# Local attention scores: the queries' remaining parts against the keys' leading parts only, two heads on the two halves of the array's rows

## Chip, cores and metric

The kernel runs on one core of a Trainium2 chip. The metric is the device time of one execution in microseconds (us). A program's time is the median of its runs; beside it stands one profiled execution, in which every instruction has its start and its length.

## What is computed

The reference is a two-layer encoder trunk over 2048 tokens of width 1024. Layer 0 mixes windowed attention (8 query heads of 64, 2 key heads, window of 128 to both sides, a sink logit and a distance bias) with a short convolution; layer 1 mixes latent attention with a gated MLP. The change lies in layer 0's windowed attention alone, in this line and the one that follows it:

```python
logits = jnp.einsum('bnqkgd,bnskd->bnkgqs', qb, kw).astype(jnp.float32) * (dh ** -0.5)
logits = logits - slopes * dist[:, :, None, None]
```

For each block n of 128 queries and each key head g, four query heads meet the keys of three blocks (384 keys; 256 for the first and the last block).

## The kernel before

**Split numbers.** A float32 value is held as two float32r parts: the leading part (a copy in float32r) and the remaining part (the difference). The helper `split` (L66 to L69) makes them, on ScalarE and VectorE. A product of two such values is made on TensorE as three matmuls (`mm3`, L78 to L80): leading with leading, leading with remaining, remaining with leading.

**Scores.** A head has only 64 numbers, so the scores are packed differently. The keys' tile `kw` holds the 64 leading rows on partitions 0 to 63 and the 64 remaining rows on partitions 64 to 127 (L397). The queries' tile `qw` holds, for each of four heads, the leading part (index a = 0) and the remaining part (a = 1), each of them twice, on both halves of the partitions (L393 to L395). One matmul over all 128 rows with a = 0 gives leading times (leading + remaining); a second one with a = 1 gives remaining times (leading + remaining), all four products. Both go into the same PSUM bank (L401 to L404):

```python
for j in range(4):
    ps = self.psB("ps")
    for a in range(2):
        nc.tensor.matmul(ps[:, :W], q[:, a, j], k[:, :W], start=a == 0, stop=a == 1)
```

The queries are the stationary operand (128 columns), the keys the moving one (W = 384 or 256 columns). VectorE then adds the distance bias while it takes the bank out to `L` (L406). `psB` has two banks.

**Stage A.** `phase_a` projects the input in 24 column tiles of weights by four chunks of 512 tokens: each such unit is 24 matmuls of 512 columns (`project`, with `mm3`). After a unit, `attend` traces the attention of one (n, g) at a time, with a priority that puts it ahead: the output matmuls of the pair two before (`att_out`, L441), the transposes of the pair one before (`att_turn`, L429), the scores of this one (`att_scores`). There are 32 pairs of (n, g). A scheduler fixes each engine's order when the program is built; an engine then runs its instructions in that order and waits where an operand or a buffer isn't ready. The SP queue issues nearly all of the stage's transfers, also in a fixed order.

**After it.** `phase_out(0)` makes the output projection of layer 0; it needs what stage A wrote to DRAM as `u0`. Layer 1 follows. None of its code changes.

Of the kernel before, what the change touches and what calls it, by code (L numbers as in the profile page):

```python
# [12 lines left out]
F32R = mybir.dt.float32r  # L13
I32 = mybir.dt.int32
AF = mybir.ActivationFunctionType
ALU = mybir.AluOpType
# [4 lines left out]
P = 128  # L21
# [33 lines left out]
class Builder:  # L55
# [116 lines left out]
    def phase_a(self):  # L172
        tc, nc, I, c, d = self.tc, self.nc, self.i, self.c, self.d
# [5 lines left out]
        sp = es.enter_context(tc.tile_pool(name="aat", bufs=1))  # L179
# [192 lines left out]
        def att_scores(n, g):  # L372
            k0 = max(0, (n - 1) * P)
            k1 = min(S, (n + 2) * P)
            W = k1 - k0
            off = k0 - (n - 1) * P
            if g == 0:
                b = blk[n] = {}
                kp = sp.tile([P, 2, 3 * P], F32, name="kp", tag="kp", bufs=1)
                self.dma(kp[:, 0, :W], d["posh"][k0:k1].partition_broadcast(P))  # L380
                self.dma(kp[:, 1, :W], d["posl"][k0:k1].partition_broadcast(P))
                dist = sp.tile([P, 3 * P], F32, name="dist", tag="dist", bufs=2)
                nc.vector.tensor_scalar(dist[:, :W], kp[:, 1, :W], posq[:, 1, n:n + 1], None, ALU.subtract)
                nc.vector.scalar_tensor_tensor(dist[:, :W], kp[:, 0, :W], posq[:, 0, n:n + 1], dist[:, :W],
                                               ALU.subtract, ALU.add)
                nc.scalar.activation(dist[:, :W], dist[:, :W], AF.Abs)
                nc.gpsimd.tensor_tensor(dist[:, :W], dist[:, :W], mask[:, off:off + W], ALU.add)
                b.update(dist=dist, W=W)
                b["o"] = sp.tile([P, 4, P], F32, name="oT", tag="oT", bufs=2)
            b = blk[n]  # L390


            q = sp.tile([P, 2, 4, P], F32R, name="qw", tag="qw", bufs=2)  # L393
            for a in range(2):
                self.dma(q[64 * a:64 * a + 64], d["q0"][64 * g:64 * g + 64, n])  # L395
            k = sp.tile([P, 3 * P], F32R, name="kw", tag="kw", bufs=2)
            self.dma(k[:, :W], d["k0"][g].rearrange("a e s -> (a e) s")[:, k0:k1])  # L397
            v = b["v", g] = sp.tile([P, 3, P], F32R, name="vw", tag="vw", bufs=4)
            self.dma(v[:, :W // P], d["v0"][k0:k1, g].rearrange("(b p) a e -> p b (a e)", p=P))
            L = b["L", g] = sp.tile([P, 4, 3 * P], F32, name="L", tag="L", bufs=2)  # L400
            for j in range(4):  # L401
                ps = self.psB("ps")
                for a in range(2):
                    nc.tensor.matmul(ps[:, :W], q[:, a, j], k[:, :W], start=a == 0, stop=a == 1)  # L404
                slope = 2.0 ** -(4 * g + j + 1)
                nc.vector.scalar_tensor_tensor(L[:, j, :W], b["dist"][:, :W], -8.0 * slope, ps[:, :W],  # L406
                                               ALU.mult, ALU.add)
            sm = sp.tile([P, 6, 4], F32, name="sm", tag="sm", bufs=3)
            nc.vector.tensor_reduce(sm[:, 0], L[:, :, :W], AX.X, ALU.max)
            nc.vector.tensor_tensor(sm[:, 0], sm[:, 0], sink8[:, 4 * g:4 * g + 4], ALU.max)  # L410
            nc.vector.tensor_scalar(sm[:, 1], sm[:, 0], -0.125, None, ALU.mult)
            nc.vector.tensor_tensor(sm[:, 2], sink[:, 4 * g:4 * g + 4], sm[:, 1], ALU.add)
            nc.scalar.activation(sm[:, 2], sm[:, 2], AF.Exp)
            for j in range(4):
                nc.scalar.activation(L[:, j, :W], L[:, j, :W], AF.Exp, bias=sm[:, 1, j:j + 1], scale=0.125,
                                     accum_out=sm[:, 3, j:j + 1])
            nc.vector.tensor_tensor(sm[:, 4], sm[:, 3], sm[:, 2], ALU.add)
            nc.vector.reciprocal(sm[:, 5], sm[:, 4])
            for j in range(4):
                nc.vector.tensor_scalar(L[:, j, :W], L[:, j, :W], sm[:, 5, j:j + 1], None, ALU.mult)  # L420
# [49 lines left out]
        def attend(limit):  # L470
            t = tick[0]
            if t >= len(groups) + 2 or (t < len(groups) and groups[t][0] >= limit):
                return False
            tick[0] += 1
            with tc.high_priority(ATTEND):
                if t >= 2:
                    att_out(*groups[t - 2])
                if 1 <= t <= len(groups):
                    att_turn(*groups[t - 1])
                if t < len(groups):  # L480
                    att_scores(*groups[t])
            return True
# [986 lines left out]
```

## Time and profile before

| | us |
|---|---|
| median of 3 runs | 2878.97 (2873.27 to 2884.52) |
| the profiled execution | 2881.51 |
| its span, first to last instruction | 2879.7 |
| TensorE busy, of the span | 2819.8 (98%) |
| VectorE busy | 1987.6 (69%) |
| ScalarE busy | 1322.2 (46%) |
| GpSimd busy | 1096.7 (38%) |

Engines: PE is TensorE's matmuls, PEld its weight loads (they run beside the matmuls), DVE VectorE, ACT ScalarE, POOL GpSimd, SPq the DMA-issuing queue of SyncE. Matmuls are pipelined and the end of each is modelled, so that the lengths of matmuls in a row overlap: what one costs is read from start to start, not from its length. In a timeline "x4" joins neighbours of one kind, and the length is that of all.

### The profile page before, as it was taken

The page shows a single profiled execution, that of the slowest core. Times are in us where ns is not written, and L with a number is a line of the kernel's source. Part 1 is how long each engine was busy: PE and PEld are TensorE (multiplying, and loading weights), DVE is VectorE, ACT ScalarE, POOL GpSimd, SP SyncE. Part 2 cuts the span into 40 slices and gives each one's busy share as a digit, 9 for nine tenths or more (in the row PEclk, how much of TensorE's full clock was granted, in tenths as well). Part 3 has the DMA queues.
Part 4 walks back from the last instruction along what each step waited for, and adds up shares of the span by engine and source line. Part 5 has one row for each costly group of instructions (what it writes and reads, how often), then busy time and mean ns, then how long its engine had stood idle before and what let it go on. Part 6 is the DMA issues. An engine that isn't in the chain of part 4 may idle for free. (4 is left out here: it accounts for less than half of the span.)

```text
span 2879.7 us, 38354 instructions
## 1 busy us (share of the span) xinstructions
PE 2819.8 (98%) x12808; PEld 2292.0 (80%) x12808; DVE 1987.6 (69%) x3957; ACT 1322.2 (46%) x2475; POOL 1096.7 (38%) x833
## 2 busy tenths in 40 slices
PE   9999999999999999999999999999999999899999
PEld 7888888888788887888887877777777776678887
DVE  4688557786655554454764789989898995666665
ACT  3545335445211111324442368888888887211111
POOL 0011000022311111120102258898899888523432
PEclk9999999999999999999999999999999999899999
DMA  7644365453733445423873333133322323433441
GB/s 233 186 139 140 124 194 166 133 142 118 219 119 119 130 136 212 148 66 128 292 268 108 106 101 76 37 72 84 84 54 61 83 69 78 139 106 114 126 123 43
DMA packets 316598, 365.26 MB, mean 127 GB/s; under 512 B 33248, under 2 KB 244368, under 8 KB 311280
## 3 DMA queue, kind: packets, MB, share of 16 engines
q1 hardware_dynamic: 249056, 295.62, 36.6%
q10 hardware_dynamic: 67344, 67.18, 7.0%
q8 instruction: 101, 1.65, 0.2%
q14 instruction: 97, 0.79, 0.1%
HBM read 238.19 MB, written 124.53 MB: 126 GB/s over the span
## 5 line engine op out<-in xcount | busy, mean ns | idle before, releaser
L1334 POOL TENSOR_TENSOR acc<-acc,ph 128x512 f32<-128x512 f32 x448 | 582.9, 1302 | 41.8 <-ACT ph L1326 10.9
L1328 DVE TENSOR_TENSOR pl<-pst,ph 128x512 fp32r<-128x512 f32 x512 | 347.0, 684 | 62.7 <-ACT ph L1326 50.0
L1196 DVE TENSOR_REDUCE mx<-pm 128x1 f32<-128x512 f32 x512 | 347.8, 682 | 27.4 <-PE pm L1195 21.1
L78 PE MATMUL pa<-xh,w 128*128 128x512 f32 x832 | 328.4, 395 | 6.0 <-ACT xh L68 6.0
L79 PE MATMUL pa<-xl,w 128*128 128x512 f32 x832 | 329.9, 397 | 0.0
L80 PE MATMUL pa<-xh,w 128*128 128x512 f32 x832 | 328.0, 394 | 0.0
L1323 ACT ACTIVATE pst<-pst 128x512 f32<-128x512 f32 x512 | 296.6, 585 | 61.2 <-PE pst L1322 29.9
L1326 ACT ACTIVATE ph<-pst 128x512 fp32r<-128x512 f32 x512 | 301.5, 595 | 31.8 <-POOL acc L1334 1.6
L78 PE MATMUL py<-wh,ou 128*128 128x512 f32 x512 | 208.3, 407 | 13.0 <-DVE ox L639 8.2
L1320 PE MATMUL pst<-mqh,mkh 97*128 97x512 f32 x512 | 205.6, 402 | 3.6 <-DVE pl L1328 1.9
L1195 PE MATMUL pm<-mkh,mqh 96*128 96x512 f32 x512 | 203.3, 398 | 4.8 <-DVE mx L1196 4.8
L647 POOL TENSOR_TENSOR ox<-ox,ln_g 128x1024 f32<-128x1024 f32 x32 | 80.4, 2514 | 334.3 <-DMA praw<-in_pT 171.6
L90 PE MATMUL pg<-wh,oht 128*128 128x512 f32 x512 | 201.1, 393 | 4.5 <-ACT oht L68 4.5
L1245 PE MATMUL px<-ph,mv 128*128 128x512 f32 x512 | 205.3, 401 | 0.0
L79 PE MATMUL py<-wl,ou 128*128 128x512 f32 x512 | 205.3, 401 | 0.0
L1321 PE MATMUL pst<-mql,mkh 96*128 96x512 f32 x512 | 204.4, 399 | 0.0
L1322 PE MATMUL pst<-mqh,mkl 96*128 96x512 f32 x512 | 203.8, 398 | 0.0
L80 PE MATMUL py<-wh,ou 128*128 128x512 f32 x512 | 203.6, 398 | 0.0
L1246 PE MATMUL py<-pl,mv 128*66 128x512 f32 x512 | 201.9, 394 | 0.8 <-DVE pl L1328 0.7
L90 PE MATMUL pg<-wl,oht 128*128 128x512 f32 x512 | 200.4, 391 | 0.0
L671 ACT ACTIVATE osg<-pg 128x512 f32<-128x512 f32 x64 | 38.3, 599 | 344.8 <-PE pg L92 333.2
L78 PEld LDWEIGHTS pa<-xh,w 128*128 128x128 f32 x832 | 157.4, 189 | 37.8 <-ACT xh L68 7.0
(370 smaller groups left out, 6255.3 us busy)
## 6 DMA issues: line engine op xcount, KB each, us to landing
ou<-u SPq DMA_DIRECT2D x96, 256.0 KB
qw<-q SPq DMA_DIRECT2D x64, 256.0 KB
x1T<-oxt ACTq DMA_DIRECT2D x64, 256.0 KB
cx<-x1T SPq DMA_DIRECT2D x16, 1024.0 KB
q<-st SPq DMA_DIRECT2D x32, 256.0 KB
u<-ua SPq DMA_DIRECT2D x32, 256.0 KB
wraw<-in_w_out SPq DMA_DIRECT2D x16, 512.0 KB
ox<-in_x SPq DMA_DIRECT2D x16, 512.0 KB
```

The lines of the kernel that those rows point to most:

```text
L78: mm(ps, ah, bh, start=start, stop=False)
L79: mm(ps, ah, bl, start=False, stop=False)
L80: return mm(ps, al, bh, start=False, stop=stop)
L90: mm(ps, a[:, 0, k], b[k][part][:, cols], start=k == 0 and part == 0, stop=False)
L1196: nc.vector.tensor_reduce(self.mx[blk][:, b, kc:kc + 1], ps, AX.X, ALU.max)
L1245: mm(x, v[:, kb, 0:P], ph, start=kb == 0, stop=kb == 15)
L1320: mm(ps, kh[0:97, ks], qh[0:97, qs], start=True, stop=False)
L1321: mm(ps, kh[0:96, ks], ql[0:96, qs], start=False, stop=False)
L1323: ex = nc.scalar.activation(ps, ps, AF.Exp, scale=scale)
L1326: nc.scalar.activation(ph, ps, AF.Copy)
L1328: behind = nc.vector.tensor_tensor(pl, ps, pf, ALU.subtract)
L1334: nc.gpsimd.tensor_tensor(acc, acc, pf, ALU.add)
```

## The change

For a pair of heads, two PSUM banks are taken together. Two full matmuls (128 rows) come first, one for each head, as before: leading queries against both parts of the keys. Then come two matmuls of 64 rows each: the first head's remaining parts on rows 0 to 63 against the keys' leading parts in `kw`, the second head's on rows 64 to 127 against a second copy of the keys' leading parts, in a new tile `kw2`. The product remaining by remaining is left out. The four are kept in this order on TensorE, and the two evictions follow. One transfer is added for each (n, g): 64 partitions of `kw2`.

```diff
             k = sp.tile([P, 3 * P], F32R, name="kw", tag="kw", bufs=2)
             self.dma(k[:, :W], d["k0"][g].rearrange("a e s -> (a e) s")[:, k0:k1])
+            k2 = sp.tile([P, 3 * P], F32R, name="kw2", tag="kw2", bufs=2)
+            self.dma(k2[64:128, :W], d["k0"][g, 0, :, k0:k1])
             v = b["v", g] = sp.tile([P, 3, P], F32R, name="vw", tag="vw", bufs=4)
...
-            for j in range(4):
-                ps = self.psB("ps")
-                for a in range(2):
-                    nc.tensor.matmul(ps[:, :W], q[:, a, j], k[:, :W], start=a == 0, stop=a == 1)
-                slope = 2.0 ** -(4 * g + j + 1)
-                nc.vector.scalar_tensor_tensor(L[:, j, :W], b["dist"][:, :W], -8.0 * slope, ps[:, :W],
-                                               ALU.mult, ALU.add)
+            for j2 in range(0, 4, 2):
+                pss = [self.psB("ps") for _ in range(2)]
+                with tc.manual_schedule(engines={mybir.EngineType.PE}):
+                    for j, ps in enumerate(pss):
+                        nc.tensor.matmul(ps[:, :W], q[:, 0, j2 + j], k[:, :W], start=True, stop=False)
+                    for j, (ps, kk) in enumerate(zip(pss, (k, k2))):
+                        r = slice(64 * j, 64 * j + 64)
+                        nc.tensor.matmul(ps[:, :W], q[r, 1, j2 + j], kk[r, :W], start=False, stop=True)
+                for j, ps in zip((j2, j2 + 1), pss):
+                    slope = 2.0 ** -(4 * g + j + 1)
+                    nc.vector.scalar_tensor_tensor(L[:, j, :W], b["dist"][:, :W], -8.0 * slope, ps[:, :W],
+                                                   ALU.mult, ALU.add)
```

## Rows read from the trace of the kernel before

**Rows 1.** The page: span, busy time of TensorE, granted clock in 40 slices.

```profile
span 2879.7 us, 38354 instructions
...
PE 2819.8 (98%) x12808; PEld 2292.0 (80%) x12808; DVE 1987.6 (69%) x3957; ACT 1322.2 (46%) x2475; POOL 1096.7 (38%) x833
...
PEclk9999999999999999999999999999999999899999
```

**Rows 2.** Windows, first to last score matmul: length, busy us (instructions), clock, DMA share, GB/s.

```profile
76.00:680.00 604.00, 601.74 (x2895) 505.55 (x2895) 442.12 (x844) 287.66 (x619) 73.54 (x69) 1.00 0.52 149
```

**Rows 3.** Waits of PE from 0 to 720 us: waiter, cause, total us, times, longest.

```profile
PE pa L78 <- ACT xh L68: 6.0, 2, 5.0
PE ps L404 <- DMA kw<-k: 2.3, 1, 2.3
```

**Rows 4.** Timeline of PE, one narrow and one wide stretch: start, length, instruction.

```profile
76.97 0.64 PE L404 MATMUL ps<-kw,qw 128*128 128x256 f32 x4
77.44 0.39 PE L80 MATMUL pa<-xh,w 128*128 128x512 f32 x1
...
134.71 0.39 PE L78 MATMUL pa<-xh,w 128*128 128x512 f32 x1
134.94 0.85 PE L404 MATMUL ps<-kw,qw 128*128 128x384 f32 x4
135.64 0.39 PE L79 MATMUL pa<-xl,w 128*128 128x512 f32 x1
135.87 0.40 PE L80 MATMUL pa<-xh,w 128*128 128x512 f32 x1
```

**Rows 5.** The score matmuls by tile: lengths in ns (min/median/max), first and last start, forms.

```profile
L404 PE MATMUL ps<-kw,qw x256: 274/336/687, 77.0 to 671.3; 128*128 128x384 f32 x112, 128*128 128x256 f32 x16
```

**Rows 6.** Timeline of PE around a block of transposes (L429).

```profile
156.10 0.28 PE L523 MATMUL cs<-ones,sqa 128*128 128x2 f32 x2
156.24 1.07 PE L429 MATMUL pt<-ident,L 128*128 128x128 f32 x8
157.07 0.48 PE L79 MATMUL pa<-xl,w 128*128 128x512 f32 x1
157.38 0.39 PE L80 MATMUL pa<-xh,w 128*128 128x512 f32 x1
157.61 0.40 PE L78 MATMUL pa<-xh,w 128*128 128x512 f32 x1
```

**Rows 7.** Timeline of PE in layer 1: matmuls of 97 and 96 rows behind 128.

```profile
1900.63 0.39 PE L1246 MATMUL py<-pl,mv 128*66 128x512 f32 x1
1900.86 0.40 PE L1320 MATMUL pst<-mqh,mkh 97*128 97x512 f32 x1
1901.10 0.40 PE L1321 MATMUL pst<-mql,mkh 96*128 96x512 f32 x1
```

**Rows 8.** Timeline of DVE: evictions of the scores (L406) and what stood between.

```profile
135.49 0.55 DVE L406 SCALAR_TENSOR_TENSOR L<-dist,ps 128x384 f32<-128x384 f32 x1 [0.26 <-PE ps L404]
135.96 1.22 DVE L69 TENSOR_TENSOR w<-w_12r,w 128x1024 fp32r<-128x1024 f32 x1
137.10 0.55 DVE L406 SCALAR_TENSOR_TENSOR L<-dist,ps 128x384 f32<-128x384 f32 x1
```

**Rows 9.** Timeline of the SP queue: start of an issue, its length, transfer.

```profile
147.35 1.09 SPq L74 DMA_DIRECT2D qw<-q  x2
148.49 0.58 SPq L74 DMA_DIRECT2D kw<-k  x1
151.12 0.56 SPq L74 DMA_DIRECT2D szw<-sza  x1
```

**Rows 10.** Timeline of PE at the end of stage A.

```profile
715.52 0.39 PE L80 MATMUL pa<-xh,w 128*128 128x512 f32 x1
715.75 4.74 PE L523 MATMUL cs<-ones,sqb 128*128 128x2 f32 x32
722.86 0.77 PE L78 MATMUL py<-wh,ou 128*128 128x512 f32 x1 [2.37 <-DMA ou<-u]
```

## The prediction

> **What bounds the kernel now.** I read the page first. TensorE is busy for 2819.8 of 2879.7 us, with its clock granted in full nearly throughout [rows 1]; no other engine comes near. Then the stretch that holds every score matmul, 76 to 680 us: PE is busy for 601.74 of 604 us at clock 1.00 [rows 2]. A busy share can hide short stalls, since the lengths of matmuls are modelled and overlap, so the waits come next: up to 720 us PE is seen waiting 6.0 us for a split of the input and 2.3 us for the keys, and for nothing else [rows 3]. So the stage is as long as TensorE's instruction stream. What is taken out of that stream is won, unless a wait takes its place; what happens on other engines costs nothing as long as PE doesn't come to wait for it. The stage's end is PE's too: projections run until 715.52, the closing column sums start right behind, and the next stage starts at 722.86, 2.37 us of it a wait for a transfer [rows 10]. A shift of PE's stream moves this end along with it.
>
> **What a score matmul costs.** From start to start, not by length. Four wide ones run from 134.94 to 135.64, so 175 ns each; four narrow ones from 76.97 to 77.44, so 117 ns each [rows 4]. Their modelled length is 336 ns at the median [rows 5], so some 161 ns of one lie over its successor. A (n, g) has eight of them; 28 of the 32 (n, g) are wide, 4 narrow.
>
> **The change, part by part.**
>
> *The leading queries' matmuls* stay as they are, four for each (n, g).
>
> *The remaining parts.* Four full matmuls become two pairs of half matmuls, with as many columns each. If the two of a pair run beside each other, a pair takes the time of one: 175 ns saved for each of 56 wide pairs, 117 ns for each of 8 narrow ones: 9.8 + 0.9 = 10.7 us. If they run one behind the other, nothing is saved: a matmul of 96 or 97 rows starts its successor 0.24 us later, just as long as one with 128 [rows 7], so fewer rows alone buy nothing. The trace of before has no matmul on a part of the rows beside another, so the term lies between 0 and -10.7 us. I take overlap, because the two share no array rows, no partitions and no bank, and what they do share, the issue and the weight loading, is short in the trace: two small matmuls with weights of their own start 0.14 us before the next kind, 70 ns each [rows 6]. In Part 3, The mechanism, of the page TensorE: Matmul & The Clock Gate, the Trainium skill says that matmuls on different row groups overlap and start about 4 ns apart; no row of before shows it, and by it the term would be within 0.3 us of its full 10.7.
>
> *One weight load more in the time of a matmul.* Eight transposes with a weight load each start within 0.83 us, 104 ns each [rows 6], and this I take for what a load needs. Two loads for a pair are 208 ns, the matmul over which they can be made lasts 175 ns, so 33 ns stick out: 64 pairs by 33 ns, +2.1 us. If the second load can't start before the first half runs, the second half starts 104 ns late, and the pair saves 71 instead of 142 ns, some 4.5 us in all; if loads hide entirely, the term is 0.
>
> *Changing the array's shape.* Going from full rows to halves and back happens once for each pair, 64 times in and 64 times out, because projections stand on both sides. The nearest rows: 97 and 96 rows behind 128 cost nothing (0.23 to 0.24 us) [rows 7]; the first projection behind a block of transposes takes 0.31 us to its successor instead of 0.23, 80 ns more [rows 6]; and if the pipeline had to run empty at each change, the 161 ns that now lie over the successor would show. So 0, 80 or 161 ns at a change. I take 80 ns once for each pair, since a change of matmul kind is nearer to this than fewer rows in the same kind: +5.1 us; the ends are 0 and 128 by 161 ns, +20.6 us.
>
> Against the change speaks the Trainium skill, TensorEngine Tiling, Key Properties: changing the tiling mode, not just the tile, drains TensorE. No row of before changes the mode, so none bears it out; it is the second rival below.
>
> *Two banks at once.* The second pair of a (n, g) needs both banks free, so two evictions of 0.55 us each must be done, where before one sufficed for the next head. Queued behind the waiting matmul on PE are projections, and everything that they feed. I cost this at nothing, because the scheduler puts projections between the pairs, as it does now (six of them, 1.4 us, fit over two evictions), and the trace shows no wait of PE for a bank [rows 3]. The cover fails where VectorE is late: in [rows 8] a weight split of 1.22 us stands between two evictions. That is the third rival.
>
> *VectorE* has the same 128 evictions: nothing.
>
> *The added transfer.* 32 issues on the SP queue, each some 0.58 us as that of `kw` [rows 9], put `vw` and whatever follows back by that much. The queue has room (nothing is issued from 149.07 to 151.12 [rows 9]), its buffer comes free with those of `kw`, and the DMA engines are 0.52 busy [rows 2]. PE waited once for `kw`, 2.3 us [rows 3]; the new tile is issued 0.6 us later but is needed two matmuls (0.35 us) later. Nothing, with 0 to +3 us as bounds, the top being that one wait come again.
>
> *Order.* A new program has a new fixed order on each engine. That can win or lose a few us at stage borders; the whole of the stage's visible waits is 8.3 us [rows 3], so I allow 4 us either way.
>
> **The sum.** -10.7 + 2.1 + 5.1 = -3.5 us. On the profiled execution's 2881.51 us that is 2878.0. That execution lies 2.5 us above the median of the runs, so against the median 2878.97 the forecast is 2875.5 us. A measurement of this kernel can tell about 0.5% from no change, 14.4 us; the forecast is well within.
>
> **The rivals.**
>
> 1. *The halves run one behind the other.* The change then doesn't do what it says: no matmul time is saved, and the change of shape stays. +5.1 us, 2884 us (2879 to 2892). For it: nothing in the trace of before shows two matmuls at once, and every form, whatever its rows, has its full price. Against it: they share no rows and no bank.
>
> 2. *Overlap, but the array runs empty at each change of shape.* -10.7 + 2.1 + 20.6 = +12.0 us, 2891 us. It turns the change into a loss from (10.7 - 2.1)/128 = 67 ns at a change. For it: the 80 ns behind the transposes show that a change of kind isn't always free. Against it: 96 rows behind 128 are free.
>
> 3. *PE waits for the second bank.* The second pair stands in PE's order where the scheduler thought both banks free; if VectorE is late by one eviction (0.55 us) in each of the 32 (n, g), that is 17.6 us, and with the forecast's -3.5 the time is 2893 us. Over +14.4 us it comes if PE waits 0.56 us for each (n, g). Against it: today's PE waits for no bank.
>
> 4. *Slower: no overlap and an array that runs empty.* +20.6 us, 2900 us. This is one mechanism, TensorE treating a half as a full matmul in another mode; at full price for the halves it passes +14.4 us from 112 ns at each of the 128 changes. For and against: as in 1 and 2 together.
>
> **How the numbers follow.** Forecast 0.45; halves in a row 0.22; overlap with emptying 0.13; waits for banks 0.10; no overlap with emptying 0.10. More than 14.4 us faster is out of the sum's reach (10.7 is its most), and only a luckier order adds to it: 0.05, taken from the forecast. More than 14.4 us slower: most of the last case (0.09), half of the waits (0.05), a small part of the second rival (0.03): 0.17. The rest, 0.78, is within 0.5%. The range reaches from full overlap with all else free, 2868, less 4 for the order, to the last case: 2864 to 2900. About 1 in 10 is left out at each end.
>
> **What the profile after would show.** *Overlap*: the two half matmuls of a pair start within some 35 ns, and the next projection starts about 0.2 us after the first; in a row, they start 175 ns apart. *Weights*: a weight load of the second half that ends behind the end of the full matmul's columns. *Change of shape*: the start of the first half stands more than 175 ns behind that of the second full matmul, or the projection after the pair takes over 0.23 us to its successor; 80 ns a pair is my term, 161 ns on both sides the rival's. *Banks*: PE waiting for DVE at the score matmuls, absent now. *The transfer*: PE waiting for `kw2`. *Through to the end*: stage A's last projection, 715.52 now, comes earlier by what the pairs save, and the later stages keep their lengths. The prediction is wrong if the score matmuls are cheaper by 10 us and the time isn't, or if stages that the change doesn't touch differ by more than 4 us.

## The result, and the profile after

The changed kernel takes 2897.62 us at the median of 4 runs (2893.79 to 2900.64), the kernel before 2876.12 beside it: ratio 1.0072, 95% interval [1.0057, 1.0088]. That is a loss of some 21 us, over the 0.5% that can be told from no change, where "no change" was forecast.

The page of the changed kernel, the lines that answer to [rows 1]:

```profile
span 2892.0 us, 38411 instructions
...
PE 2833.7 (98%) x12808; PEld 2277.8 (79%) x12808; DVE 1994.8 (69%) x3957; ACT 1322.6 (46%) x2475; POOL 1098.8 (38%) x833
...
PEclk9999999999999999999999999999999999899999
```

TensorE is as full as before, its clock as high, with the same number of matmuls; its weight loads are busy 14 us less. The waits of PE explain nothing either. Those up to 740 us, as in [rows 3]:

```profile
PE pa L78 <- ACT xh L68: 6.3, 3, 5.1
PE pvt L313 <- ACT st L310: 1.4, 1, 1.4
```

There is no wait for a bank and none for `kw2` or `kw`. Yet the stage is longer. Its end on PE, as in [rows 10]:

```profile
732.89 0.39 PE L80 MATMUL pa<-xh,w 128*128 128x512 f32 x1
733.12 3.63 PE L531 MATMUL cs<-ones,sqb 128*128 128x2 f32 x32
740.69 0.77 PE L78 MATMUL py<-wh,ou 128*128 128x512 f32 x1 [3.94 <-DVE wl L69]
```

The column sums begin at 733.12 instead of 715.75, 17.4 us later, and layer 0's output projection 17.8 us later. So the loss arises in stage A.

Not all of the 17.4 us can be the half matmuls'. The score matmuls in the changed kernel:

```profile
L408 PE MATMUL ps<-kw,qw x128: 275/332/422, 80.0 to 694.1; 128*128 128x384 f32 x112, 128*128 128x256 f32 x16
L411 PE MATMUL ps<-kw,qw x128: 379/440/443, 80.3 to 694.3; 64*128 64x384 f32 x112, 64*128 64x256 f32 x16
```

The first score starts at 80.0 us, where the kernel before has 77.0 [rows 5]. So 3 us are gone before any half runs; on the other side the wait of 2.3 us for the keys [rows 3] is gone from the stretch of the scores. What the halves cost is better read against a full-row kernel with the same frame (run 2 below).

Of the two profiled executions the one after is 12.3 us longer, 2893.79 against 2881.51: from the column sums to the end it is 2164 us before and 2159 after, and 2159 to 2168 in those experiments below whose attention ends with the stage, so the stages behind, which the change doesn't touch, differ by that much from one program to the next.

Where the loss arises shows in TensorE's timeline around one pair of heads (L408 are the full matmuls, L411 the halves). A passage from full rows to half rows and back is called a visit from here on.

```profile
140.06 0.40 PE L78 MATMUL pa<-xh,w 128*128 128x512 f32 x1
140.30 0.33 PE L408 MATMUL ps<-kw,qw 128*128 128x384 f32 x1
140.56 0.44 PE L411 MATMUL ps<-kw,qw 64*128 64x384 f32 x2
140.93 0.50 PE L79 MATMUL pa<-xl,w 128*128 128x512 f32 x1
141.27 0.40 PE L80 MATMUL pa<-xh,w 128*128 128x512 f32 x1
141.50 0.85 PE L449 MATMUL po<-PT,vw 128*128 128x512 f32 x3
```

The two halves, joined in one row, last 0.44 us together, and one alone has a median of 440 ns (line L411 above): they run beside each other. In the trace's own records the starts of a pair are 3 to 4 ns apart. But from the full matmul to the halves it is 0.26 us, where 0.17 is its own time [rows 4]; from the halves to the next projection 0.37; and from that to its successor 0.34, where it is 0.23 elsewhere [rows 6]. The weight loads of the same place say why:

```profile
140.07 0.19 PEld L408 LDWEIGHTS ps<-kw,qw 128*128 128x128 f32 x1
140.56 0.19 PEld L411 LDWEIGHTS ps<-kw,qw 64*128 64x128 f32 x2 [0.30 <-issue]
140.93 0.19 PEld L79 LDWEIGHTS pa<-xl,w 128*128 128x128 f32 x1 [0.18 <-issue]
141.04 0.19 PEld L80 LDWEIGHTS pa<-xh,w 128*128 128x128 f32 x1
141.27 0.66 PEld L449 LDWEIGHTS po<-PT,vw 128*128 128x128 f32 x3
```

Elsewhere a load starts a whole matmul ahead of its use, as the one at 140.07 does for the matmul at 140.30, and the one at 141.04 for that at 141.27. Here the halves' loads start only at 140.56, together with the halves and 0.07 us before the full matmul's modelled end, and the next projection's only at 140.93, 0.07 us before the halves' end. So it is at all 71 visits of this trace, wide and narrow: the first load behind a change starts 1 to 3 ns ahead of the matmul that needs it. No load crosses the change of shape, in either direction. The list of waits does show it, not for PE but for PEld, in a row that the kernel before doesn't have (19.7 us over 68 loads of halves):

```profile
PEld ps L411 <- issue: 19.7, 68, 0.4
```

Taking 0.104 us for a load [rows 6]: going in, 0.26 - 0.17 = 0.09 us pass beyond the full matmul's own time until the halves' load starts, and I take this for the array running empty; then 0.10 of loading stands bare (it lies in the halves' recorded length, 0.44 instead of 0.33). Going out, it is 0.37 - 0.10 - 0.17 = 0.10 us of emptying and the next load's 0.11. That is 0.39 to 0.40 us for one visit, against 0.174 us that a pair saves. The sum and the starts of the loads are read from the trace; the split between emptying and loading is an estimate from these rows.

### The profile page after: what moved, and what is told of

Its sections match the earlier page's. It is cut to its first block, busy times and chain, and to the rows that moved or that the text cites. A ratio compares the mean times of both kernels' runs of the same rounds, so it can differ in the third digit from the quotient of the medians.

```text
span 2892.0 us, 38411 instructions
## 1 busy us (share of the span) xinstructions
PE 2833.7 (98%) x12808; PEld 2277.8 (79%) x12808; DVE 1994.8 (69%) x3957; ACT 1322.6 (46%) x2475; POOL 1098.8 (38%) x833
## 5 line engine op out<-in xcount | busy, mean ns | idle before, releaser
L78 PE MATMUL py<-wh,ou 128*128 128x512 f32 x512 | 208.0, 406 | 17.8 <-DVE ox L647 11.5
```

What stands on the lines that cost most here:

```text
L78: mm(ps, ah, bh, start=start, stop=False)
```

## The experiments

The theory: the price lies in the change of shape, once for each visit. The rivals: the two banks, the order or the added transfer make TensorE wait; or each half matmul is dear by itself.

**1. Full rows in the changed kernel's frame.**

```diff
-                    for j, (ps, kk) in enumerate(zip(pss, (k, k2))):
-                        r = slice(64 * j, 64 * j + 64)
-                        nc.tensor.matmul(ps[:, :W], q[r, 1, j2 + j], kk[r, :W], start=False, stop=True)
+                    for j, ps in enumerate(pss):
+                        nc.tensor.matmul(ps[:, :W], q[:, 1, j2 + j], k[:, :W], start=False, stop=True)
```

> The changed kernel with its two banks at once, its fixed order of four matmuls and its transfer of kw2, but the remaining queries' matmuls on all 128 rows again, against both parts of the keys. Theory (changes of the array's shape cost about 0.4 us a pair of halves, 64 pairs): without half matmuls the loss goes, the time is that of before, ratio 0.999 to 1.002, and the last projection of stage A ends near 716 us. Rival (taking two banks at once, or the added transfer, makes TensorE wait): the loss stays, ratio 1.006 to 1.008, last projection near 733 us.

Measured: 2893.68 us, ratio 1.0052 [1.0039, 1.0064]. By its number that is the rival's. But the time went at another place. This run's first score starts only at 88.8 us, 11.8 us later than in the kernel before, and up to 80 us PE waited for weights (second row), which it does neither before [rows 3] nor after:

```profile
PE pvt L313 <- ACT st L310: 3.6, 1, 3.6
PE pa L78 <- ACT w L68: 3.1, 1, 3.1
```

The SP queue of this run:

```profile
28.86 2.53 SPq L74 DMA_DIRECT2D kw<-k  x4
...
50.75 0.59 SPq L74 DMA_DIRECT2D w_4r<-in_w  x1
...
63.57 0.55 SPq L74 DMA_DIRECT2D w_5r<-in_w  x1
```

In the kernel before, `w_5r` is issued at 30.84. With no reader, `kw2` never holds its buffer, so its loads (shown as `kw` too; digits are left off the names) were free to go early, and at attention's priority they went ahead of the weights. The control was at fault, and its time tells nothing of the change.

**2. The control mended.** `kw2` is a full copy of `kw`, and the second head's remaining matmul reads it.

```diff
-            self.dma(k2[64:128, :W], d["k0"][g, 0, :, k0:k1])
+            self.dma(k2[:, :W], d["k0"][g].rearrange("a e s -> (a e) s")[:, k0:k1])
...
-                        r = slice(64 * j, 64 * j + 64)
-                        nc.tensor.matmul(ps[:, :W], q[r, 1, j2 + j], kk[r, :W], start=False, stop=True)
+                        nc.tensor.matmul(ps[:, :W], q[:, 1, j2 + j], kk[:, :W], start=False, stop=True)
```

> The full-row control again, with what was wrong in the first one mended: there kw2 had no reader, so its buffers were free at once and its loads were issued ahead of weight loads (TensorE lost some 12 us before 80 us). Here kw2 is a full copy of kw (128 partitions) that the second head's remaining matmul reads, all on 128 rows, in the changed kernel's two banks and order. Theory (the loss is the change of shape): as before, ratio 0.998 to 1.003, excess of TensorE's stream in stage A, over matmuls at their start-to-start times, some 18 us as in before, last projection near 716 to 720 us. Rival (two banks, order or transfer): ratio 1.005 to 1.008.

Measured: 2878.67 us, ratio 1.0002 [0.9993, 1.0011]. The end of its stage A:

```profile
714.22 0.39 PE L80 MATMUL pa<-xh,w 128*128 128x512 f32 x1
714.46 3.63 PE L530 MATMUL cs<-ones,sqb 128*128 128x2 f32 x32
```

Two banks at once, the fixed order and a transfer twice as large as the change's cost nothing that shows in the time (the interval reaches from -0.07% to +0.11%). So the loss belongs to the matmuls on half rows. Against this kernel, whose first score starts at 79.3 us, the changed kernel's stage A is 18.7 us longer (733.12 against 714.46), 0.7 of it ahead of the first score and some 17.9 behind it.

**3. Full rows without `kw2`**: the edit of 1, and

```diff
-            k2 = sp.tile([P, 3 * P], F32R, name="kw2", tag="kw2", bufs=2)
-            self.dma(k2[64:128, :W], d["k0"][g, 0, :, k0:k1])
```

> Full rows, two banks at once and the fixed order, without kw2 and its transfer. Theory: as before, ratio 0.998 to 1.003. If the first control's loss was the two banks after all and not the unread kw2, it is there again: 1.004 to 1.006.

Measured: 2878.53 us, ratio 1.0008 [0.9997, 1.0020]. It agrees, and shows that the first control's loss was the unread tile's.

**4. One half instead of two.**

```diff
-                    for j, (ps, kk) in enumerate(zip(pss, (k, k2))):
-                        r = slice(64 * j, 64 * j + 64)
-                        nc.tensor.matmul(ps[:, :W], q[r, 1, j2 + j], kk[r, :W], start=False, stop=True)
+                    nc.tensor.matmul(pss[0][:, :W], q[:, 1, j2], k[:, :W], start=False, stop=True)
+                    nc.tensor.matmul(pss[1][:, :W], q[64:128, 1, j2 + 1], k2[64:128, :W], start=False, stop=True)
```

> The changed kernel with only the second head's remaining part on 64 rows; the first head's is a full matmul ahead of it. As many changes of shape, but half as many half matmuls, and nothing beside them. Theory (the halves overlap fully, the price belongs to the change of shape): 64 matmuls of 175 or 117 ns more, +10.7 us over the changed kernel, ratio to before 1.010 to 1.012. Rival (the price belongs to each half matmul, about 0.2 us each over a full one, without overlap): half of them gone, ratio 1.003 to 1.004.

Measured: 2906.13 us, ratio 1.0092 [1.0079, 1.0105]; stage A's column sums begin at 742.88, 9.8 us after those of the changed kernel. One visit with a lone half:

```profile
150.38 0.34 PE L409 MATMUL ps<-kw,qw 128*128 128x384 f32 x1
150.65 0.43 PE L410 MATMUL ps<-kw,qw 64*128 64x384 f32 x1
151.01 0.50 PE L78 MATMUL pa<-xh,w 128*128 128x512 f32 x1
151.35 0.39 PE L79 MATMUL pa<-xl,w 128*128 128x512 f32 x1
```

0.27, 0.36 and 0.34 us: a lone half takes what a pair takes. The second half is free, and the price is the visit's. Fewer half matmuls made the kernel slower, which the price for each half excludes. The median lies somewhat under the theory's 1.010 to 1.012: the changed kernel turned out to make more than 64 visits and to overlap fewer than 64 pairs (below run 8). And of the 9.8 us some 2.3 are again gone before the first score, which starts at 82.3 here.

**5. The halves apart**, full, half, full, half.

```diff
-                    for j, ps in enumerate(pss):
-                        nc.tensor.matmul(ps[:, :W], q[:, 0, j2 + j], k[:, :W], start=True, stop=False)
                     for j, (ps, kk) in enumerate(zip(pss, (k, k2))):
                         r = slice(64 * j, 64 * j + 64)
+                        nc.tensor.matmul(ps[:, :W], q[:, 0, j2 + j], k[:, :W], start=True, stop=False)
                         nc.tensor.matmul(ps[:, :W], q[r, 1, j2 + j], kk[r, :W], start=False, stop=True)
```

> The changed kernel with the four matmuls of a pair in the order full, half, full, half: the same instructions, twice as many changes of shape, no overlap. Theory (0.4 us for each change in and out, and the halves' overlap lost): a pair takes some 1.49 us instead of 0.93, 64 times 0.57 is +36 us over the changed kernel, ratio to before 1.018 to 1.021. Rival (price of each half matmul, not of the change): only the overlap is lost, if there was one, 0 to +11 us over the changed kernel, ratio 1.007 to 1.011.

Measured: 2935.17 us, ratio 1.0192 [1.0178, 1.0205], as the theory has it: with twice the visits the loss is more than doubled.

**6. Four heads in one visit**, with two banks borrowed from tag C.

```diff
-            for j2 in range(0, 4, 2):
-                pss = [self.psB("ps") for _ in range(2)]
+            for j2 in (0,):
+                pss = [self.psB("ps"), self.psB("ps"), self.psC("ps"), self.psC("ps")]
...
-                    for j, (ps, kk) in enumerate(zip(pss, (k, k2))):
-                        r = slice(64 * j, 64 * j + 64)
+                    for j, (ps, kk) in enumerate(zip(pss, (k, k2, k, k2))):
+                        r = slice(64 * (j % 2), 64 * (j % 2) + 64)
```

> The changed kernel with all four heads of a (n, g) together: four full matmuls into four banks (two of tag B, two of tag C), then the four half matmuls, so one change in and out where there were two. Theory: 32 times 0.4 us less, -12.7 us against the changed kernel, ratio to before 1.000 to 1.004; no better than that, since one change (0.40 us) costs what two overlapped pairs save (0.35 us). Rival (price of each half matmul): as the changed kernel, 1.006 to 1.008. If holding four banks makes TensorE wait, that shows as idle time of PE ahead of the score matmuls, transposes or output matmuls.

Measured: 2954.70 us, ratio 1.0260 [1.0239, 1.0281]: neither. Its scores end here:

```profile
L411 PE MATMUL ps<-kw,qw x128: 277/437/687, 80.4 to 804.7; 64*128 64x384 f32 x112, 64*128 64x256 f32 x16
```

The last projection starts at 713.83, and the scores ran on until 804.7 with little to cover them (before, they end at 671.3 [rows 5]). I put this down to the banks taken from transposes and outputs, which this run alone doesn't show; the question of the price needed banks of its own.

**7 and 8. Four banks of their own**: the kernel of 6 with these edits, and for the control (8) also with the edit of 2, full rows.

```diff
-        self.c_bufs = 3
+        self.a_bufs, self.b_bufs, self.c_bufs = 2, 4, 2
...
+        self.a_bufs, self.b_bufs, self.c_bufs = 3, 2, 3
+        self.ps_open("psx")
...
-                pss = [self.psB("ps"), self.psB("ps"), self.psC("ps"), self.psC("ps")]
+                pss = [self.psB("ps"), self.psB("ps"), self.psB("ps"), self.psB("ps")]
```

> Four heads together again, four full matmuls and four halves, but with four banks of their own: in stage A tag A has 2 banks, B 4, C 2, and a new pool with 3, 2 and 3 opens for the stages behind. Attention then need not share tag C's banks, which put it off beyond the stage's projections in the run before. Theory (0.40 us for each change in and out, 32 of them): +2 us against full rows in the same banks (the next kernel); rival (a price of some 0.2 us for each half matmul): +15 us against it.

> The same four banks with all eight score matmuls on 128 rows (kw2 a full copy, read by the second and fourth head): the control for the four banks. Two projection banks instead of three could cost some us; ratio to before 0.999 to 1.004. By the theory the kernel with halves in these banks is 2 us (0 to 4) slower than this one, by the rival some 15 us.

Measured: with halves 2924.93 us, ratio 1.0162 [1.0148, 1.0177]; with full rows 2912.08, 1.0116 [1.0103, 1.0130]. The second misses its own expectation, 0.999 to 1.004: attention falls behind the projections in these banks too, where tag C still has one bank less than in the kernel before. Its last projection starts at 709.20, its last scores far behind:

```profile
L410 PE MATMUL ps<-kw,qw x128: 277/337/422, 84.9 to 732.5; 128*128 128x384 f32 x112, 128*128 128x256 f32 x16
```

The difference between the two is 12.9 us, near the rival's 15 and not the theory's 2. The timeline of the kernel with halves shows what I had overlooked:

```profile
149.96 0.68 PE L408 MATMUL ps<-kw,qw 128*128 128x384 f32 x3
150.57 0.43 PE L411 MATMUL ps<-kw,qw 64*128 64x384 f32 x1
150.93 0.50 PE L449 MATMUL po<-PT,vw 128*128 128x512 f32 x1
151.27 0.60 PE L437 MATMUL pt<-ident,L 128*128 128x128 f32 x4
151.80 0.62 PE L411 MATMUL ps<-kw,qw 64*128 64x384 f32 x3
152.35 0.50 PE L80 MATMUL pa<-xh,w 128*128 128x512 f32 x1
```

The fixed order holds for the score matmuls among themselves; other attention work may stand between them. The four halves were torn apart, and TensorE made 53 visits instead of 32. The changed kernel has the same flaw in small: 71 visits for 64 pairs, of which 57 stayed together.

So I counted visits. For each kernel I took the starts of PE's matmuls from 76 us to the last score, and from each interval took off the matmul's own time (0.227 us for 512 columns, 0.174 for 384, 0.118 for 256, 0.107 for a transpose, some 0.02 for a column sum), leaving out waits over 0.6 us. What remains is the stream's excess; with the time that overlapped pairs saved, and less the excess of the full-row control in the same banks (run 2, and run 8 for the four banks), it is what the visits cost. Run 6 has no control in its banks and is left out. (Run 2 expected some 18 us of excess; that counted the whole stage with its start, where it has 16.9.)

| kernel | excess, us | saved by overlap, us | control's excess, us | visits | us a visit |
|---|---|---|---|---|---|
| changed | 25.6 | 9.6 | 7.7 | 71 | 0.388 |
| one half (4) | 32.3 | 0 | 7.7 | 64 | 0.386 |
| apart (5) | 57.9 | 0 | 7.7 | 128 | 0.392 |
| four banks (7) | 25.7 | 9.0 | 14.3 | 53 | 0.385 |
| adjacent (9) | 21.1 | 10.7 | 7.7 | 64 | 0.378 |
| pairs twice (10) | 10.4 | 21.4 | 7.7 | 64 | 0.378 |

The price is the same whether a visit holds one half or four, and whether there are 53 visits or 128. Before any visits are counted the controls differ among themselves by about 1 us, some 0.015 us a visit. At the changed kernel's 0.388 us, 53 visits less the 9.0 us saved make 11.6 us, against the 12.9 measured between the two kernels with four banks: the theory stands, and my expectation was wrong in the number of visits. Narrow visits, of 256 columns, show the same intervals over their matmuls' own time as wide ones: 0.09 us going in, 0.20 behind the halves and 0.11 behind the next projection.

**9. Pairs kept together**, by a higher priority for the scores.

```diff
-                with tc.manual_schedule(engines={mybir.EngineType.PE}):
+                with tc.high_priority(2 * ATTEND), tc.manual_schedule(engines={mybir.EngineType.PE}):
```

> The changed kernel with a higher priority for its score matmuls, so that nothing else comes between the two halves of a pair. In the changed kernel's trace TensorE goes 71 times to half rows, since 7 of the 64 pairs were torn apart; counted over four runs each such visit cost 0.385 to 0.392 us over the matmuls' own time. Theory: 64 to 66 visits, 57 to 64 pairs overlapped, some 2 to 4 us less than the changed kernel, ratio 1.005 to 1.007, still a loss. A rival by which the torn pairs were the main cause: within 0.002 of before.

Measured: 2895.03 us, ratio 1.0063 [1.0047, 1.0079], with 64 visits and 64 overlapped pairs. The median is 2.6 us under the changed kernel's, as expected, though the two intervals overlap. By the table the torn pairs cost some 4.5 us of excess, a small part.

**10. Each pair twice in a visit**, in the kernel of 9.

```diff
-                    for j, (ps, kk) in enumerate(zip(pss, (k, k2))):
-                        r = slice(64 * j, 64 * j + 64)
-                        nc.tensor.matmul(ps[:, :W], q[r, 1, j2 + j], kk[r, :W], start=False, stop=True)
+                    for last in (False, True):
+                        for j, (ps, kk) in enumerate(zip(pss, (k, k2))):
+                            r = slice(64 * j, 64 * j + 64)
+                            nc.tensor.matmul(ps[:, :W], q[r, 1, j2 + j], kk[r, :W], start=False, stop=last)
```

> As the kernel with the higher priority, but each pair of halves is issued twice, so that the remaining product is counted twice. It measures a pair that follows another within one visit. If weight loads hide beside half matmuls as they do beside full ones, a pair adds 174 ns: +11 us over the kernel with the pair once. If a load can't be made while half matmuls run, it adds 104 ns more, 280 ns in all: +17 to +18 us, and the second pair starts some 0.28 us behind the first.

Measured: 2906.72 us, ratio 1.0100 [1.0079, 1.0121], 11.7 us over the kernel of 9. A visit with two pairs:

```profile
143.50 0.42 PE L408 MATMUL ps<-kw,qw 128*128 128x384 f32 x1
143.86 0.62 PE L412 MATMUL ps<-kw,qw 64*128 64x384 f32 x4
144.40 0.50 PE L79 MATMUL pa<-xl,w 128*128 128x512 f32 x1
144.74 0.39 PE L80 MATMUL pa<-xh,w 128*128 128x512 f32 x1
```

From the halves to the projection it is 0.54 us, where one pair has 0.37: the second pair adds 0.17. The second pair does start 0.28 us behind the first, as one outcome had it, but the first pair's bare load is in that. The loads of this visit:

```profile
143.85 0.30 PEld L412 LDWEIGHTS ps<-kw,qw 64*128 64x128 f32 x4 [0.19 <-issue]
144.40 0.19 PEld L79 LDWEIGHTS pa<-xl,w 128*128 128x128 f32 x1 [0.25 <-issue]
```

By the trace's own records the second pair's two loads begin at 143.96, 0.17 us ahead of their matmuls (144.14), while the first pair runs. The projection's load waits again until the projection itself starts. Within a visit loads hide as they do among full matmuls; only the change itself lays them bare.

No version beats the kernel before; runs 2 and 3, with full rows in two banks, equal it.

## Why the prediction was wrong

**What bounds the kernel** was right. TensorE's stream sets the stage, and a loss in it went through: 17.4 us in stage A, some 21 in the median time. The few us between the two are less than the 6.9 us by which the runs of the changed kernel spread.

**Overlap** was right. The halves start 3 to 4 ns apart and the second is free (run 4). Of the 10.7 us, 9.6 were had, since 7 pairs were torn apart; that the fixed order allows this I had not seen. The offset of about 4 ns between starts that the Trainium skill gives, in Part 3, The mechanism, of TensorE: Matmul & The Clock Gate, agrees with the 3 to 4 ns.

**The second weight load** was sized at 33 ns a pair, +2.1 us, and costs nothing. I had put the two loads one behind the other, 208 ns; they run beside each other (in the changed kernel two in 0.19 us, at 140.56), and in run 10 two loads hide beside a pair.

**Changing the array's shape** is the step that failed. I took 80 ns once for each pair, from the row behind a block of transposes, and 161 ns at each of two changes as the most, +20.6 us. Measured are 0.38 to 0.39 us for a visit, 0.19 at each change, five times the term and over its upper end; with 71 visits that is 27.5 us instead of 5.1. I bounded only the emptying of the array, by the part of a matmul that lies over its successor. That part of the price was too high, if anything: 0.09 to 0.10 us at a change show. What was missing are the weight loads. Those of the full matmuls hide by being made one matmul ahead, and I assumed that cover for the loads at the change too, in the very step that asked what a load costs, without asking if a load may be made ahead across a change. The projection behind the transposes, on which I leaned, was misread. In the kernel before:

```profile
157.04 0.27 PE L429 MATMUL pt<-ident,L 128*128 128x128 f32 x1
157.04 0.19 PEld L79 LDWEIGHTS pa<-xl,w 128*128 128x128 f32 x1
```

This projection starts at 157.07 [rows 6], 0.03 us behind the last transpose, and its load only at 157.04. So the 80 ns are most of one bare load, queued behind those of the transposes, and nothing of emptying shows. The row held one of the parts that I missed, and I read it as the price of a change of kind.

The sum with measured sizes: -9.6 us of overlap, and 71 visits at the 0.378 to 0.392 us of the other kernels, make +17.2 to +18.2 us; against the full-row control of run 2 the stretch of the scores grew by 17.9. That stage A grew by nearly the same 17.4 against the kernel before is partly chance, since there a start of the scores 3 us later and a wait of 2.3 us that went away nearly offset each other.

**Order** was allowed 4 us either way. The later first score, 3 us, lies within that, and what moved it stays open; the stages behind differ by 5 us between the two profiled executions, a little more than I gave them.

**The second rival** (overlap, but the array runs empty) was the mechanism, given 0.13 and +12.0 us; with the loads it is the whole result. The rule of the Trainium skill, in TensorEngine Tiling (Array Packing), Key Properties, that a change of the tiling mode drains TensorE, fits the 0.09 to 0.10 us that pass at each change here. I gave this rival a small chance because no row of before had a change of mode. But an absent row is no evidence against a rule, and the case needed only 67 ns at a change to turn into a loss.

**The other rivals** fell: halves in a row (run 4), waits for banks (runs 2 and 3, and no such wait after), and with the first the slower case that combined it with emptying. That case's 2900 us lay near the measured time for another reason: it had no overlap and too low a price.

**Faster by 0.5%** had been excluded rightly: the saving's limit is 10.7 us.

## What to carry to other kernels

Row packing pays by the visit, not by the matmul: with 384 columns a pair saves 0.174 us and a visit costs 0.38 to 0.39, so by these numbers a visit must hold three such pairs before it pays, which no run tried. In this kernel each pair holds two PSUM banks until the visit is over, and four banks for the scores made even the full-row kernel 1.2% slower (run 8). Before packing halves between full matmuls, count the changes of shape, and check in the built order that nothing else stands within a visit. When a step leans on weight loads that hide, ask whether they can still be made ahead at that place; and in a control, give every added tile a reader, or its transfer moves to another place in the queue.

## What the runs showed of the hardware

- Two matmuls on different halves of the rows, into different banks, start 3 to 4 ns apart and take the time of one; a lone half takes as long as the pair (run 4). Their weight loads run beside each other too.
- Between full and half rows no weight load is made ahead: a visit costs 0.38 to 0.39 us, by estimate about half of it emptying and half two bare loads of 0.10 to 0.11 us. Between 128, 97 and 96 rows nothing of it shows [rows 7].
- Within a visit loads hide again: a second pair adds 0.17 us (run 10).
